# Moving the head sums of the RWKV bonus behind the prep, with the products parked in DRAM

## The chip, the core and the metric

The kernel runs on one core of a Trainium2 chip. TensorE (PE) multiplies, VectorE (DVE) and ScalarE (ACT) do elementwise work and evict the accumulators, GpSimd (POOL) and SyncE (SP) here mostly start DMAs; ACT starts DMAs as well, from the same queue that holds its compute instructions. Each engine takes its instructions strictly in the order in which they were laid down, so an instruction that waits holds up everything behind it on that engine. The metric is device microseconds of one execution; lower is better.

## The reference, cut to what matters

The block has an RWKV-7 time mixing branch, a gated recurrent branch, cross-attention and a gated convolutional FFN, for 512 positions of width 1024. The change touches one line of the time mixing, the `bonus`:

```python
p = p + (token_shift(p) - p) * mu
r, k, v = p[..., :c0], p[..., c0:c1], p[..., c1:c2]
...
k = k * (1.0 + (a - 1.0) * k_a)
...
y = rwkv7_recurrence(r, decay, k, v, -kk, kk * a)
mean = jnp.mean(y, axis=-1, keepdims=True)
var = jnp.mean(jnp.square(y - mean), axis=-1, keepdims=True)
y = ((y - mean) * lax.rsqrt(var + LNX_EPS)).reshape(bsz, s, A_WIDTH) * lnx_g + lnx_b
bonus = jnp.sum(r * k * r_k, axis=-1, keepdims=True) * v
return (y + bonus.reshape(bsz, s, A_WIDTH)) * g
```

Per head of 64 channels and per position, the products r\*k\*r_k are added up to one number, which scales v. Eight heads lie in four pairs, each pair being a tile of 128 channels (partitions) by 512 positions.

## The kernel before

Activations lie with channels on partitions and positions along the free axis. Every dense product is done in three matmuls of a split in high and low parts (L160, L161, L162), so a block of 128 output columns with 1024 inputs is 24 matmuls 128x512, written to an accumulator `in_ps`. There are 38 such blocks in the input projection: the first 14 make r, k, v and the low-rank inputs of the time mixing, then come 16 gate blocks (`in_ps22` on, evicted by ACT into `gs`, stored to `dG`), then 8 blocks of the other branch. Their weights stream from DRAM on SP's queue (`win_r`), and ACT (`win_h`, L114) and DVE (`win_l`, L115) split them; three split blocks are held at a time, so `win_h` of a block waits until PE is done with the block three earlier. Three `in_ps` accumulators are held at a time.

Between these blocks the scheduler, which lays each engine's order down when the program is built, sets the time mixing's own work:

- **Prep**, for each of the four head pairs j: `prep` (two small products psw and psa, then sigmoid, a scan `L`, exponentials), `prep2` (norm of k through a head sum `ss`, then the decayed rows `AK` and `KBt`), `scores` (32 matmuls 64x128, L605, in four accumulators, evicted by eight DVE operations L609 and L610 into `BZ` and `AK`, and half of it stored to `dM` by SP), and `bonus`. psw, psa, ss, the four `sc` and `bo` take turns in four accumulator slots (`prw`).
- `bonus(j)` before the change, L585 to L591: DVE multiplies r, r_k and k in place in `pr`; `sum_exact` (L154 to L157) splits the product on ACT (`bo_h`) and DVE (`bo_l`) and adds over each head with two matmuls against a block matrix of ones into `bo`; DVE multiplies by v; ACT adds `lnx_b`; a DMA from ACT's queue stores the tile in `dBo`, where the group norm reads it much later (L821).
- **The block inverse**: two DMAs bring the diagonal blocks of all heads from `dM` back as `Nm` (L654), and 31 steps of two DVE operations each (L660, L661) invert them in `Zt`; the result goes through DRAM (`dZt`, `dZ`) into `ZA` and `BZ`; then come small matmuls `zh` and `zo`, and the scan over eight chunks. PE goes through gate blocks meanwhile. The tiles of the inverse lie in the memory that the prep's pool `pp` has just given back.

A third stream rides along: POOL starts 512 KB accumulating DMAs `dS` in DRAM for the later FFN (L425), each released by a given matmul of a given block (`sum_behind`): one each behind the first products of blocks `in_ps27`, `in_ps28` and `in_ps29`, none in `in_ps30` to `in_ps37`.

Of the kernel before, what the change touches and what calls it, by code (L numbers as in the profile page):

```python
# [9 lines left out]
F32 = mybir.dt.float32  # L10
F32R = mybir.dt.float32r
AF = mybir.ActivationFunctionType
ALU = mybir.AluOpType
# [4 lines left out]
P = 128  # L18
T = 512
# [6 lines left out]
NPAIR = NH // 2  # L26
# [27 lines left out]
def hybrid_block_kernel(ctx: ExitStack, tc: tile.TileContext, xT_d, mT_d, pv_d, cst_d, win_d, wk_d, wv_d,  # L54
                        lup_d, gup_d, rga_d, rgx_d, wba_d, wbb_d, wmix_d, wq_d, wo_d, wfi_d, wfo_d, out_d):
    nc = tc.nc
    V, S, PE = nc.vector, nc.scalar, nc.tensor
# [12 lines left out]
    def mm_ps(name):  # L70
        return pmm.tile([P, T], F32, tag="mm", name=name)

    def rw_ps(name, pool=None, tag="rw", **kw):
        return (pool or prw).tile([P, T], F32, tag=tag, name=name, **kw)
# [9 lines left out]
    def par(name, i, n=1):  # L84
        o = PV[name][0]
        return pv[:, o + i:o + i + n]
# [63 lines left out]
    def sum_exact(ps, blocks, src, pool, tag, name):  # L150

        hi = pool.tile(list(src.shape), F32R, tag=tag, name=f"{name}_h", bufs=2)
        lo = pool.tile(list(src.shape), F32R, tag=tag, name=f"{name}_l", bufs=2)
        S.copy(hi, src)  # L154
        V.tensor_tensor(lo, src, hi.bitcast(F32), ALU.subtract)
        PE.matmul(ps, blocks, hi, start=True, stop=False)
        PE.matmul(ps, blocks, lo, start=False, stop=True)  # L157
# [36 lines left out]
    bonesr = cp.tile([P, P], F32R, name="bonesr")  # L194
# [72 lines left out]
    with tc.tile_pool(name="p0", bufs=1, reuse_waits="tile") as p0:  # L267
# [36 lines left out]
        for m in range(KB):  # L304
            ps = rw_ps(f"k_ps{m}") if 3 <= m < 6 else mm_ps(f"k_ps{m}")
# [93 lines left out]
    dBo = dr.tile([4, P, T], F32, name="dBo")  # L399
# [82 lines left out]
    vT = pa.tile([P, NPAIR, T], F32, name="vT")  # L482
# [4 lines left out]
    tp = tp_ctx.enter_context(tc.tile_pool(name="tp", bufs=1, reuse_waits="tile"))  # L487
# [28 lines left out]
    def inproj(i):  # L516
        ps = mm_ps(f"in_ps{i}")
        dense(ps, uin, lambda kb: (h2[:, 0, kb, :], h2[:, 1, kb, :]), KB, NSUM.get(i, 0))
        return ps

    def evac_shift(ps, blk, out):
        q = pp.tile([P, T], F32, tag="q", name=f"q{blk}", bufs=2)
        V.tensor_copy(q[:, 0:1], qb[:, blk:blk + 1])
        S.activation(q[:, 1:T], ps[:, 0:T - 1], AF.Identity, scale=par("mu", blk), bias=par("b_in", blk))
        V.scalar_tensor_tensor(out, ps, omu[:, blk:blk + 1], q, ALU.mult, ALU.add)  # L525
# [17 lines left out]
    def prep(j):  # L543
        sl = slice(j * P, (j + 1) * P)
        psw, psa = rw_ps(f"psw{j}"), rw_ps(f"psa{j}")
        for i, ps in enumerate((psw, psa)):
            PE.matmul(ps, lhi[:, i, sl], pwa[i], start=True, stop=False)
            PE.matmul(ps, llo[i][:, sl], pwa[i], start=False, stop=True)
        L = pp.tile([P, T], F32, tag="L", name=f"L{j}")
        tab(L, psw, AF.Sigmoid, bias=par("w0", j))  # L550
        at = pp.tile([P, T], F32, tag="at", name=f"at{j}")
        tab(at, psa, AF.Sigmoid, bias=par("a0", j))
        V.tensor_tensor_scan(L, smask, L, 0.0, ALU.mult, ALU.add)
        Pp = pp.tile([P, NC, HD + 1], F32, tag="Pp", name=f"Pp{j}")
        V.memset(Pp[:, :, 0:1], 1.0)
        tab(Pp[:, :, 1:], L.rearrange("p (c t) -> p c t", t=HD), AF.Exp, scale=-C0)
        tab(L, L, AF.Exp, scale=C0)
        V.tensor_copy(PC[:, j, :], Pp[:, :, HD])
        return at, L, Pp

    def prep2(j, pk, pr, at, Pi, Pp):
        c3 = lambda a: a.rearrange("p (c t) -> p c t", t=HD)
        kk = pp.tile([P, T], F32, tag="kk", name=f"kk{j}")
        S.activation(kk, pk, AF.Copy, scale=par("k_k", j))
        sq = pp.tile([P, T], F32, tag="q", name=f"sq{j}", bufs=2)
        S.activation(sq, kk, AF.Square)
        ps = rw_ps(f"ss{j}")
        sum_exact(ps, bonesr, sq, tp, "xb", f"ss{j}")
        tab.rsqrt(sq, ps, 1.0, eps[:, 2:3])
        V.scalar_tensor_tensor(kk, sq, 1e12, kk, ALU.min, ALU.mult)  # L570
        jc = slice(j * NC, (j + 1) * NC)
        for e in range(2):
            hs = half[e]
            V.scalar_tensor_tensor(AK[hs, e, jc, 0:HD], c3(kk)[hs], -1.0, Pp[hs, :, 0:HD], ALU.mult, ALU.mult)
        V.tensor_tensor(kk, kk, at, ALU.mult)
        V.tensor_tensor(KBt[:, j, 1::2, :], c3(kk), c3(Pi), ALU.mult)
        S.activation(at, at, AF.Identity, scale=par("k_a", j), bias=oka[:, j:j + 1])
        V.tensor_tensor(pk, pk, at, ALU.mult)
        V.tensor_tensor(KBt[0:HD, j, 2::2, :], c3(pk)[0:HD], c3(Pi)[0:HD], ALU.mult)
        V.tensor_tensor(KBt[HD:P, j, 0:2 * NC:2, :], c3(pk)[HD:P], c3(Pi)[HD:P], ALU.mult)  # L580
        for e in range(2):
            hs = half[e]
            V.tensor_tensor(AK[hs, e, jc, HD:P], c3(pr)[hs], Pp[hs, :, 1:], ALU.mult)

    def bonus(j, pk, pr):  # L585
        V.scalar_tensor_tensor(pr, pr, par("r_k", j), pk, ALU.mult, ALU.mult)
        ps = rw_ps(f"bo{j}")
        sum_exact(ps, bonesr, pr, tp, "xb", f"bo{j}")
        V.tensor_tensor(pr, ps, vT[:, j, :], ALU.mult)
        S.activation(pr, pr, AF.Identity, bias=par("lnx_b", j))  # L590
        nc.scalar.dma_start(dBo[j], pr)  # L591

# [3 lines left out]
    def scores(j):  # L598
        for e in range(2):
            hs, oh = half[e], half[1 - e]  # L600
            for cg in range(2):
                ps = rw_ps(f"sc{j}_{e}_{cg}")
                i0 = j * NC + cg * 4
                for i in range(4):
                    PE.matmul(ps[:, i * P:(i + 1) * P], kb_cols(j, e, cg * 4 + i), AK[hs, e, i0 + i, :],  # L605
                              start=True, stop=True)
                p3 = ps.rearrange("p (c t) -> p c t", t=P)
                m3 = scmask.unsqueeze(1).to_broadcast([P, 4, P])
                V.tensor_tensor(BZ[hs, i0:i0 + 4, :], p3[hs], m3[hs], ALU.mult)  # L609
                V.tensor_tensor(AK[oh, e, i0:i0 + 4, :], p3[oh], m3[oh], ALU.mult)  # L610
            with tc.high_priority(offset=1000000):
                nc.sync.dma_start(dM[e * 32 + j * NC:e * 32 + (j + 1) * NC].rearrange("i s t -> s i t"),
                                  BZ[hs, j * NC:(j + 1) * NC, 0:HD])

    def gate_block(b):
        ps = inproj(22 + b)
        sg = tp.tile([P, T], F32, tag="st", name=f"gs{b}", bufs=2)
        tab(sg, ps, AF.Sigmoid, bias=par("b_in", 22 + b))
        nc.scalar.dma_start(dG[b], sg)

    for jp in range(2):
        js = (2 * jp, 2 * jp + 1)
        pks, prs = {}, {}
        for j in js:
            pks[j] = pp.tile([P, T], F32, tag="pk", name=f"pk{j}", bufs=2)
            evac_shift(inproj(4 + j), 4 + j, pks[j])
        for j in js:
            prs[j] = pp.tile([P, T], F32, tag="pr", name=f"pr{j}", bufs=3)
            evac_shift(inproj(j), j, prs[j])
        for j in js:  # L630
            evac_shift(inproj(8 + j), 8 + j, vT[:, j, :])
        for j in js:
            if j == 3:
                for i in IN_REST[:NEARLY]:
                    gate_block(i - 22)
            at, L, Pp = prep(j)
            prep2(j, pks[j], prs[j], at, L, Pp)
            scores(j)
            bonus(j, pks[j], prs[j])

    pp_ctx.close()
    pq_ctx = ExitStack()
    pq = pq_ctx.enter_context(tc.tile_pool(name="pq", bufs=1, reuse_waits="tile"))
    YB = pq.tile([P, 4, T], F32, name="YB")


    with tc.tile_pool(name="pz", bufs=1, reuse_waits="tile") as pz:
# [216 lines left out]
    def px_scan(b, xb, ga, gx):  # L864
# [5 lines left out]
        V.tensor_tensor(xb, xb, gx, ALU.mult)  # L870
        V.tensor_tensor_scan(YB[:, b, :], ga, xb, 0.0, ALU.mult, ALU.add)

    def py_block(b):
        ps = inproj(18 + b)
        ge = tp.tile([P, T], F32, tag="st", name=f"ge{b}", bufs=2)
        with tc.high_priority():
            tab(ge, ps, AF.Gelu_apprx_tanh, bias=par("b_in", 18 + b))
            V.tensor_tensor(YB[:, b, :], YB[:, b, :], ge, ALU.mult)

# [26 lines left out]
    for b in range(4):  # L906
        yb = YB[:, b, :]
        with tc.high_priority():
# [17 lines left out]
    for m in range(KB):  # L926
        ga = pm.tile([P, T], F32, tag="ga", name=f"gta{m}")
# [26 lines left out]
    for m in range(KB):  # L954
        xin = pm.tile([P, T], F32, tag="xin", name=f"xin{m}")
        nc.scalar.dma_start(xin, xT_d[:, m, :])
        ps = mm_ps(f"mix_ps{m}")
# [23 lines left out]
    pk = pk_ctx.enter_context(tc.tile_pool(name="pk", bufs=1, reuse_waits="tile"))  # L981
# [73 lines left out]
    pr = ctx.enter_context(tc.tile_pool(name="pr", bufs=1, side="right", reuse_waits="tile"))  # L1055
# [17 lines left out]
    for m in order:  # L1073
        ps = mm_ps(f"co_ps{m}")
# [343 lines left out]
```

## Time and profile before

| | |
|---|---|
| median of 3 runs | 911.82 us (911.26 to 913.13) |
| the profiled execution: its own time | 909.73 us |
| its span, first to last instruction | 908.0 us |
| PE busy | 890.5 us, 98% |
| DVE busy | 687.4 us, 76% |
| ACT busy | 510.4 us, 56% |
| granted TensorE clock, mean | 0.998 |

The median is 2.09 us above the profiled execution's own time, and that is 1.73 us above its span. A row of the timeline gives start, duration, engine, line, operation, output<-inputs, and in brackets idle time of the engine before it with what ended it. A matmul's shown duration overlaps the next one's, so the distance between two starts says more than the duration.

### The profile page before, as it was taken

How to read it: one execution, taken by the hardware profiler on the slowest of the kernel's cores; microseconds unless marked ns; L12 is line 12 of the kernel's file. 1: busy time of each engine (PE TensorE's matmuls, PEld its weight loads, DVE VectorE, ACT ScalarE, POOL GpSimd, SP SyncE). 2: the span in 40 equal slices, each digit the busy share in tenths (PEclk: the TensorE clock that was granted, in tenths of full speed). 3: DMA queues.
4: the chain of work that ended last, by engine and by line, in shares of the span. 5: the costliest groups of instructions: out<-in, count | busy, mean ns of one | idle time of the engine just before them, and what ended most of it. 6: DMA issues, size and time to landing. Idle time of an engine off the chain costs nothing. (4 is left out here: it accounts for less than half of the span.)

```text
span 908.0 us, 15914 instructions
## 1 busy us (share of the span) xinstructions
PE 890.5 (98%) x6218; PEld 776.1 (85%) x6218; DVE 687.4 (76%) x1096; ACT 510.4 (56%) x779; POOL 129.3 (14%) x159
## 2 busy tenths in 40 slices
PE   7999999999999999999999999999999999999996
PEld 6988877788877777887887778999999999999996
DVE  7884598776957585776565568788998888999674
ACT  6674675542236675234454446765665556767663
POOL 0102222010011212001112211111111111201100
PEclk9999999999999999999999999999999999999999
DMA  8878899667499749858788868898989998998963
GB/s 276 277 263 230 186 237 208 179 165 206 139 205 246 167 106 194 258 180 223 210 243 190 177 152 185 240 273 247 280 249 290 258 316 251 248 277 222 269 197 93
DMA packets 102411, 200.07 MB, mean 220 GB/s; under 512 B 25344, under 2 KB 36736, under 8 KB 102272
## 3 DMA queue, kind: packets, MB, share of 16 engines
q1 hardware_dynamic: 69504, 119.75, 41.0%
q0 software_dynamic: 25504, 67.38, 36.8%
q10 hardware_dynamic: 7328, 11.92, 3.9%
q8 instruction: 49, 0.80, 0.3%
q14 instruction: 26, 0.21, 0.1%
HBM read 187.75 MB, written 77.59 MB: 292 GB/s over the span
## 5 line engine op out<-in xcount | busy, mean ns | idle before, releaser
L126 ACT CAST wfi_h<-wfi_r 128x1024 fp32r<-128x1024 f32 x77 | 81.0, 1052 | 76.8 <-PE fx_ps L161 21.1
L160 PE MATMUL in_ps<-hT,win_h 128*128 128x512 f32 x304 | 121.9, 402 | 0.8 <-DVE pr L525 0.7
L162 PE MATMUL in_ps<-hT,win_l 128*128 128x512 f32 x304 | 120.8, 398 | 0.0
L161 PE MATMUL in_ps<-hT,win_h 128*128 128x512 f32 x304 | 120.6, 398 | 0.0
L127 DVE TENSOR_TENSOR wfi_l<-wfi_r,wfi_h 128x1024 fp32r<-128x1024 f32 x77 | 94.0, 1221 | 23.5 <-ACT wfi_h L126 23.3
L425 POOL DMA_DIRECT2D dS<-in_wfi x66 | 66.5, 1044 | 267.0 <-PE in_ps L160 132.4
L114 ACT CAST win_h<-win_r 128x1024 fp32r<-128x1024 f32 x38 | 39.8, 1048 | 71.9 <-PE in_ps L161 70.9
L115 DVE TENSOR_TENSOR win_l<-win_r,win_h 128x1024 fp32r<-128x1024 f32 x38 | 46.4, 1221 | 32.6 <-ACT win_h L114 32.5
L160 PEld LDWEIGHTS in_ps<-hT,win_h 128*128 128x128 f32 x304 | 57.0, 187 | 15.6 <-DVE pr L525 1.1
L161 PEld LDWEIGHTS in_ps<-hT,win_h 128*128 128x128 f32 x304 | 57.0, 188 | 14.0 <-issue 0.7
L162 PEld LDWEIGHTS in_ps<-hT,win_l 128*128 128x128 f32 x304 | 57.0, 187 | 13.9 <-issue 0.2
L461 POOL DMA_DIRECT2D dOs<-in_wfo x54 | 39.9, 804 | 186.0 <-PE fx_ps L160 50.9
L1245 DVE TENSOR_TENSOR wfo_l<-wfo_r,wfo_h 128x1024 fp32r<-128x1024 f32 (+1 forms) x39 | 47.2, 1210 | 13.6 <-ACT wfo_h L1244 13.5
L1244 ACT CAST wfo_h<-wfo_r 128x1024 fp32r<-128x1024 f32 (+1 forms) x39 | 40.4, 1038 | 28.2 <-PE oyz_ps L161 9.8
L161 PE MATMUL fx_ps<-hr,wfi_h 128*128 128x256 f32 x176 | 49.7, 282 | 0.0
L162 PE MATMUL fx_ps<-hr,wfi_l 128*128 128x256 f32 x176 | 49.7, 282 | 0.0
L160 PE MATMUL ox_ps<-go,wfo_h 128*128 128x256 f32 x176 | 49.6, 282 | 0.1
L160 PE MATMUL fyz_ps<-hq,wfi_h 128*128 128x256 f32 x176 | 49.3, 280 | 0.4 <-ACT p L1173 0.4
L160 PE MATMUL fx_ps<-hq,wfi_h 128*128 128x256 f32 x176 | 49.5, 281 | 0.0
L160 PE MATMUL fx_ps<-hr,wfi_h 128*128 128x256 f32 x176 | 49.4, 281 | 0.0
L162 PE MATMUL ox_ps<-go,wfo_l 128*128 128x256 f32 x176 | 49.3, 280 | 0.0
L161 PE MATMUL ox_ps<-go,wfo_h 128*128 128x256 f32 x176 | 49.3, 280 | 0.0
(418 smaller groups left out, 2727.8 us busy)
## 6 DMA issues: line engine op xcount, KB each, us to landing
dS<-in_wfi POOLq DMA_DIRECT2D x66, 512.0 KB, 8.4
wfi_r<-dS SPq DMA_DIRECT2D x44, 512.0 KB, 6.9
win_r<-in_win SPq DMA_DIRECT2D x38, 512.0 KB, 5.0
wfi_r<-in_wfi SPq DMA_DIRECT2D x33, 512.0 KB, 5.6
dS<-dS POOLq DMA_DIRECT2D x22, 512.0 KB, 5.7
dOs<-in_wfo POOLq DMA_DIRECT2D x12, 512.0 KB, 7.8
wv_r<-in_wv SPq DMA_DIRECT2D x8, 512.0 KB, 4.9
dG<-gs ACTq DMA_DIRECT2D x16, 256.0 KB, 2.6
```

The lines of the kernel that those rows point to most:

```text
L114: S.copy(hi[:, o:o + n], raw[:, o:o + n])
L115: V.tensor_tensor(lo[:, o:o + n], raw[:, o:o + n], hi[:, o:o + n].bitcast(F32), ALU.subtract)
L126: S.copy(hi, raw)
L127: V.tensor_tensor(lo, raw, hi.bitcast(F32), ALU.subtract)
L160: first = PE.matmul(ps, lh, rh, start=start, stop=False, **kw)
L161: PE.matmul(ps, lh, rl, start=False, stop=False, **kw)
L162: PE.matmul(ps, ll, rh, start=False, stop=stop, **kw)
L425: return lambda: nc.gpsimd.dma_start(s(out), src, **kw)
L461: yield lambda k=k, w=w, src=src: nc.gpsimd.dma_start(dO[n, m][:, k * P:(k + w) * P], src, **kw)
L1244: S.copy(hi[:, :n], raw[:, :n])
L1245: V.tensor_tensor(lo[:, :n], raw[:, :n], hi[:, :n].bitcast(F32), ALU.subtract)
```

## The change

`bonus` is cut in two. `bonus_terms(j)` stays in the prep: DVE's product, and then a DMA from ACT's queue that stores the bare product in `dBo[j]`. The new `bonus(j)` is called for all four pairs after the prep's pool is closed and ahead of the inverse: a DMA from ACT's queue brings the product back into a new tile `bt` (two buffers, tag "ga", which the prep's low-rank weights `llo` hold until the last psw and psa), and then the same sum, product with v, bias and store as before follow. So four stores and four loads of 256 KB are added; the number of matmuls and of DVE and ACT computations stays the same. As `bt` has two buffers, the load of `bt2` waits until the final store from `bt0` has landed, and `bt3` until that from `bt1` has.

```diff
-    def bonus(j, pk, pr):
+    def bonus_terms(j, pk, pr):
+
         V.scalar_tensor_tensor(pr, pr, par("r_k", j), pk, ALU.mult, ALU.mult)
+        nc.scalar.dma_start(dBo[j], pr)
+
+    def bonus(j):
+        bt = tp.tile([P, T], F32, tag="ga", name=f"bt{j}", bufs=2)
+        nc.scalar.dma_start(bt, dBo[j])
         ps = rw_ps(f"bo{j}")
-        sum_exact(ps, bonesr, pr, tp, "xb", f"bo{j}")
-        V.tensor_tensor(pr, ps, vT[:, j, :], ALU.mult)
-        S.activation(pr, pr, AF.Identity, bias=par("lnx_b", j))
-        nc.scalar.dma_start(dBo[j], pr)
+        sum_exact(ps, bonesr, bt, tp, "xb", f"bo{j}")
+        V.tensor_tensor(bt, ps, vT[:, j, :], ALU.mult)
+        S.activation(bt, bt, AF.Identity, bias=par("lnx_b", j))
+        nc.scalar.dma_start(dBo[j], bt)
...
             scores(j)
-            bonus(j, pks[j], prs[j])
+            bonus_terms(j, pks[j], prs[j])
 
     pp_ctx.close()
     pq_ctx = ExitStack()
     pq = pq_ctx.enter_context(tc.tile_pool(name="pq", bufs=1, reuse_waits="tile"))
     YB = pq.tile([P, 4, T], F32, name="YB")
+    for j in range(NPAIR):
+        bonus(j)
```

The diff moves instructions all through the prep, since the scheduler lays the order anew. Three places matter. The first is PE at the end of block `in_ps29`, after the last pair's scores (`sc3`). Before, the last bonus sum (`bo3`) was over long ahead of this place:

```order
L160 MATMUL in_ps28_2735<-hT2_0_89,win_h20_2738 128x512
L156 MATMUL bo3_1727<-bo3_h_1728,bonesr_80 128x512
L161 MATMUL in_ps28_2735<-hT2_1_90,win_h20_2738 128x512
L162 MATMUL in_ps28_2735<-hT2_0_89,win_l20_2739 128x512
L160 MATMUL in_ps28_2735<-hT2_0_89,win_h20_2738 128x512
L161 MATMUL in_ps28_2735<-hT2_1_90,win_h20_2738 128x512
L162 MATMUL in_ps28_2735<-hT2_0_89,win_l20_2739 128x512
L157 MATMUL bo3_1727<-bo3_l_1729,bonesr_80 128x512
```

Now the sum of pair 2 begins right at the end of `in_ps29`, and that of pair 3 nine matmuls later:

```order
L162 MATMUL in_ps29_2782<-hT2_0_89,win_l21_2786 128x512
L156 MATMUL bo2_1732<-bo2_h_1733,bonesr_80 128x512
L160 MATMUL in_ps30_2817<-hT2_0_89,win_h22_2820 128x512
L161 MATMUL in_ps30_2817<-hT2_1_90,win_h22_2820 128x512
L157 MATMUL bo2_1732<-bo2_l_1734,bonesr_80 128x512
L162 MATMUL in_ps30_2817<-hT2_0_89,win_l22_2821 128x512
L160 MATMUL in_ps30_2817<-hT2_0_89,win_h22_2820 128x512
L161 MATMUL in_ps30_2817<-hT2_1_90,win_h22_2820 128x512
L162 MATMUL in_ps30_2817<-hT2_0_89,win_l22_2821 128x512
L160 MATMUL in_ps30_2817<-hT2_0_89,win_h22_2820 128x512
L156 MATMUL bo3_1744<-bo3_h_1745,bonesr_80 128x512
```

Pairs 0 and 1 have moved from the prep to just behind `sc3` (bo0 at once, the second matmul of bo1 in `in_ps28`), so six of the eight bonus matmuls that stood ahead of `sc3` are now behind it.

The second place is ACT from the split of `win_h22` on, in the changed kernel (`gs5`, `gs6`, `gs7` are the evictions of blocks `in_ps27`, `in_ps28`, `in_ps29`; "DMA" rows are DMAs that ACT issues):

```order
L237 ACTIVATE gs5_2744<-in_ps27_2712,pv_75 128x512
L596 ACTIVATE bt0_1706<-bt0_1706,pv_75 128x512
L625 DMA dG_712<-gs5_2744 128x512
L597 DMA dBo_713<-bt0_1706 128x512
L596 ACTIVATE bt1_1718<-bt1_1718,pv_75 128x512
L114 CAST win_h23_2854<-win_r23_2852 128x1024
L597 DMA dBo_713<-bt1_1718 128x512
L592 DMA bt2_1730<-dBo_713 128x512
L237 ACTIVATE gs6_2779<-in_ps28_2747,pv_75 128x512
L625 DMA dG_712<-gs6_2779 128x512
L592 DMA bt3_1742<-dBo_713 128x512
L154 CAST bo2_h_1733<-bt2_1730 128x512
```

What moved: two stores and two loads now stand in ACT's order ahead of the split `bo2_h`, which PE needs; before, one store stood in this stretch.

The third is DVE where the inverse begins. Before, its steps followed one another from the first; now the product of pair 3's sum with v stands behind the second step:

```order
L595 TENSOR_TENSOR bt2_1730<-bo2_1732,vT_745 128x512
L155 TENSOR_TENSOR bo3_l_1746<-bt3_1742,bo3_h_1745 128x512
L668 TENSOR_TENSOR zz_1760<-Zt_1758,Nm_1757 128x1
L669 TENSOR_REDUCE Zt_1758<-zz_1760 128x1
L668 TENSOR_TENSOR zz_1760<-Zt_1758,Nm_1757 128x4
L669 TENSOR_REDUCE Zt_1758<-zz_1760 128x2
L595 TENSOR_TENSOR bt3_1742<-bo3_1744,vT_745 128x512
L668 TENSOR_TENSOR zz_1760<-Zt_1758,Nm_1757 128x9
```

So the third and all later steps of the inverse stand behind the bonus of pair 3.

## Prediction

> **What bounds the kernel now.** I read the page first, then the stretches of the time mixing, then who waits for whom on PE.
>
> ```profile
> span 908.0 us, 15914 instructions
> PE 890.5 (98%) x6218; PEld 776.1 (85%) x6218; DVE 687.4 (76%) x1096; ACT 510.4 (56%) x779; POOL 129.3 (14%) x159
> ```
>
> In the windows the columns are length, then busy time (and count) of PE, PEld, DVE, ACT, POOL, then granted clock, DMA share and GB/s.
>
> ```profile
> 100.00:120.00 20.00, 19.45 (x101) 15.95 (x100) 15.71 (x23) 14.45 (x19) 3.75 (x4) 1.00 0.87 210
> 120.00:140.00 20.00, 19.24 (x96) 14.88 (x95) 18.96 (x33) 13.50 (x18) 6.04 (x6) 1.00 0.97 219
> 140.00:160.00 20.00, 19.48 (x85) 15.10 (x84) 16.69 (x26) 13.55 (x18) 4.45 (x5) 1.00 0.92 205
> 160.00:180.00 20.00, 19.77 (x102) 15.93 (x101) 16.30 (x24) 10.73 (x16) 0.00 (x0) 1.00 0.66 193
> 180.00:200.00 20.00, 20.00 (x103) 16.29 (x102) 16.68 (x23) 9.40 (x12) 1.87 (x2) 1.00 0.54 130
> 200.00:220.00 20.00, 20.00 (x88) 16.05 (x87) 10.10 (x31) 6.55 (x8) 1.14 (x1) 1.00 0.92 238
> ```
>
> PE is the bound from end to end. In these windows it idles only in the prep, 2.06 us from 100 to 180, and from 180 to 220, where the bonus now goes, not at all, while DVE and ACT have room there (10.10 and 6.55 of 20). The number of matmuls doesn't change, so the time changes only by what PE waits less or more. The same matmul cadence holds throughout:
>
> ```profile
> 187.21 0.39 PE L161 MATMUL in_ps<-hT,win_h 128*128 128x512 f32 x1
> 187.44 0.39 PE L162 MATMUL in_ps<-hT,win_l 128*128 128x512 f32 x1
> 187.75 3.68 PE L605 MATMUL sc<-AK,KBt 64*128 64x128 f32 x32
> 191.36 0.50 PE L160 MATMUL in_ps<-hT,win_h 128*128 128x512 f32 x1
> ```
>
> One 128x512 matmul starts 0.233 us after another, a block of 24 takes 5.6 us, and the last pair's scores (sc3) start at 187.75 and hold PE 3.6.
>
> **The waits in the prep that can go.**
>
> ```profile
> 119.30 0.47 PE L156 MATMUL bo<-bo_h,bonesr 128*128 128x512 f32 x1 [0.55 <-DVE AK L610]
> 133.74 0.50 PE L160 MATMUL in_ps<-hT,win_h 128*128 128x512 f32 x1 [0.67 <-DVE pr L525]
> 144.75 0.49 PE L157 MATMUL bo<-bo_l,bonesr 128*128 128x512 f32 x1 [0.35 <-DVE bo_l L155]
> 145.41 0.50 PE L160 MATMUL in_ps<-hT,win_h 128*128 128x512 f32 x1 [0.17 <-DVE pk L525]
> 171.49 0.50 PE L157 MATMUL bo<-bo_l,bonesr 128*128 128x512 f32 x1 [0.23 <-DVE bo_l L155]
> ```
>
> The brackets add up to 1.97; since a shown duration of 0.4 overlaps the next start by 0.16, each hides up to 0.16 more, so about 2.7 in all. The first is a wait for an accumulator slot that a score eviction gives back: in the new order psw of pair 1 stands at that spot and waits for the same slot, so it stays (0.65), and ss of pair 1 comes right behind psa and waits for the third slot, about 0.7 by the spacing of two evictions (0.7 each). The waits at 133.74 and 145.41 are for accumulators that DVE, nearly full there (18.96 of 20), evicts late; without two bo_l and two products with v (about 0.65 each) DVE comes earlier, and I leave 0.3 of those 1.1. The two on bo_l go. So 2.7 plus some 0.7 of smaller slips becomes 0.65 + 0.7 + 0.3, rounded: **-2.1 us** (bounds -0.8, if the slots only pass the waits on, and -3.4, if all goes).
>
> By this PE is at sc3 at 187.75 - 2.1 + 0.7 = 186.4: six bonus matmuls fewer stand ahead of it and nine of in_ps27 more, three matmuls of 0.233. Is DVE there in time? Its chain for pair 3 starts with psw, now about 3.5 earlier (2.1, and six matmuls fewer ahead of it), takes bo0_l in between (0.65), and at3 has slipped behind win_h21 on ACT, which waits for PE; I get KBt at 185.8, 0.6 ahead. A miss would cost up to 1; I take 0.
>
> **The bonus beside the inverse.** Behind sc3 the rows that price it are these, of DVE and ACT:
>
> ```profile
> 189.30 0.68 DVE L609 TENSOR_TENSOR BZ<-sc,cst 64x512 f32<-64x512 f32 x1
> 194.19 0.68 DVE L610 TENSOR_TENSOR AK<-sc,cst 64x512 f32<-64x512 f32 x1
> 196.01 1.23 DVE L115 TENSOR_TENSOR win_l<-win_r,win_h 128x1024 fp32r<-128x1024 f32 x1 [0.28 <-ACT win_h L114]
> 198.49 0.69 DVE L589 TENSOR_TENSOR pr<-bo,vT 128x512 f32<-128x512 f32 x1 [0.64 <-PE bo L157]
> 194.93 1.05 ACT L114 CAST win_h<-win_r 128x1024 fp32r<-128x1024 f32 x1 [7.44 <-PE in_ps L161]
> 195.89 0.61 ACT L154 CAST bo_h<-pr 128x512 fp32r<-128x512 f32 x1
> 199.21 0.73 ACT L590 ACTIVATE pr<-pr,pv 128x512 f32<-128x512 f32 x1 [2.13 <-DVE pr L589]
> ```
>
> The eight evictions (189.30 to 194.87) start 1.4 earlier less pr3's product that now stands ahead of them: they end at 193.0. DVE then does bt0's product (to 193.7), win_l22 (1.23, to 194.9) and bo1_l (to 195.6). PE, after sc3 at 190.0, two bo0, three in_ps, bo1_h and 18 in_ps, is at bo1's second matmul at 195.4: **+0.4** with the hand-over (0 to 1.0). It then has 9 + 24 matmuls and reaches bo2's first at 203.7.
>
> bo2_h on ACT needs the load of bt2, and that waits for bt0's store to land. bt0's product done at 193.7, bias on ACT to 194.4, store issued at about 195.2; bt1's store behind win_h23, which waits for PE to end in_ps28 (197.9), at about 199.0. How long do 256 KB on ACT's queue take here? These are issues of the windows 196:198, 199:201 and 202:206 (kind, queue, count, KB, us to landing), the two POOL rows that start dS, and the queues' shares in 198:202 and 202:206:
>
> ```profile
> dG<-gs ACTq DMA_DIRECT2D x1, 256.0 KB, 7.5
> dBo<-pr ACTq DMA_DIRECT2D x1, 256.0 KB, 6.7
> dG<-gs ACTq DMA_DIRECT2D x1, 256.0 KB, 7.0
> Nm<-dM SPq DMA_DIRECT2D x1, 256.0 KB, 13.9
> ...
> 195.66 1.16 POOL L425 DMA_DIRECT2D dS<-in_wfi  x1 [8.68 <-PE in_ps L160]
> 201.78 1.14 POOL L425 DMA_DIRECT2D dS<-in_wfi  x1 [4.96 <-PE in_ps L160]
> ...
> q0 software_dynamic: 230, 0.46, 98.5%
> q10 hardware_dynamic: 8, 0.02, 1.2%
> ...
> q1 hardware_dynamic: 1828, 0.74, 66.3%
> q10 hardware_dynamic: 278, 0.51, 33.7%
> ```
>
> A dS (q0) holds nearly all of the engines for some 4 us; ACT's queue (q10) stands still and then shares with Nm. The dS are tied to PE (first matmul of in_ps28 and in_ps29), so they come 3 earlier in the new kernel, at 192.5 and 198.6, and so does Nm, at 195.6. The new stores and loads fall into the same crowd as the three rows above. With about 7 each, bt0's store lands at 202 to 203 and bt2's load at about 208.6; bo2_h takes 0.61, and PE goes on at 209.3 instead of 203.7: **+5.4**. Bounds: 0, with transfers as short as this row, from 170:180, where no dS runs,
>
> ```profile
> dBo<-pr ACTq DMA_DIRECT2D x1, 256.0 KB, 2.0
> ```
>
> and +9.5, with 9 each as the longest dS of this stretch (9.2 in its issue row). I take 5.4 since the new transfers lie in the crowd, not beside it. A page of the Trainium skill, "DMA: Bandwidth & Descriptors", section "Queues, rings and completion order", says that each engine goes round-robin between the queues that have work, packet by packet. The trace doesn't agree for 198 to 202, where dG and dBo were queued and q10 got 1.2%. By that rule both transfers would be much shorter than 7 and most of the +5.4 would go; the sum goes by the rows.
>
> bt3's load goes out when bt1's store has landed (205 to 206) and lands at 210 to 211; ACT does bo2_h, win_h24, gs7 first and has bo3_h at about 211.9, PE comes to it at 211.4: **+0.5** (0 to 3). Waiting behind bt2 and bt3 on ACT are gs6 and gs7 (accumulators for in_ps31 and later) and win_h24 (needed for in_ps32): PE, itself standing, needs them more than 8 us later, so 0.
>
> **The inverse.** The first step ran at 212.45 once Nm had landed; PE's first zh, which needs ZA from it, is this row:
>
> ```profile
> 212.45 0.16 DVE L660 TENSOR_TENSOR zz<-Zt,Nm 128x1 f32<-128x1 f32 x1 [3.22 <-DMA Nm<-dM]
> 266.45 1.19 PE L687 MATMUL zh<-ZA,BZ 32*32 32x32 f32 x32
> ```
>
> Zh had no idle ahead of it, so the slack was 0 or more. The third step (zz of 9) began 0.8 after the first, at 213.2. Now it waits for bt3's product: PE's last bo3 at 214.2, plus 0.5 and 0.69, 215.5, or 2.3 later. PE itself is 4.2 later and meets zh three matmuls (0.7) earlier in its order, so the inverse gains 1.2 of slack: **0** (0 to 2, if Nm with 1 MB more beside it lands 3 later than I think). What follows is the same work on a saturated PE.
>
> **Sum:** -2.1 + 0.4 + 5.4 + 0.5 = +4.2. The profiled execution's 909.73 (span 908.0 + 1.73 around it) becomes 913.9; the three runs' median lies 2.09 above that execution, so I forecast 911.82 + 4.2 = **916.0 us**.
>
> **Rivals.** (1) *The transfers are short.* Stores and loads of 2.0: bt0's store lands at 197.2, bt2 is issued at 199.1, lands at 201.1, bo2_h is done at 201.8, ahead of PE's 203.7; bt3 likewise. Then only -2.1 + 0.4 is left: 910.1, not slower. For it: the 2.0 row, and that DMAs of ACT go out a little earlier against the dS; against it: three rows of 6.7 to 7.5 at this spot. It decides from the point where store and load together take under 8 us. (2) *The crowd is worse,* 9 each with 1 MB added beside Nm: +9.5 in place of 5.4 and +1 more on bo3: +9.3, 921.1. (3) *The prep gains nothing,* the slots and DVE's order passing each wait on to the next instruction, or KBt late for sc3 (at3 behind win_h21): +6.3, 918.1. (4) *The inverse is late:* Nm lands past 216 and zh waits 2: 918.
>
> **Chances.** Forecast (a wait of 3 to 8 at bo2 and bo3) 0.60, own range 913 to 918.5; rival 1 0.20; rivals 2, 3 and 4 together 0.20. A measurement here tells some 0.2% (1.8 us) from no change. Faster by more: half of rival 1 and a little of better prep, 0.13. Within: the other half and the forecast's low end, 0.22. Slower: 0.65. Range 910.0 to 920.0, from rival 1 to the edge of rival 2.
>
> **What would show it.** PE idle in 100 to 180 down from 2.06 to about 1, no row of bo there. On PE one wait of 3 to 8 us ahead of a bo row L156 released by ACT's bo_h, near 209, with ACT's own idle ahead of bo_h released by a DMA bt<-dBo. bt loads and stores in 195 to 212 with 6 us or more to landing. The inverse's third step 2 to 3 us later and no idle ahead of zh. I am wrong if PE has no idle over 1 us in 195 to 215, if the loads land in under 4, or if the time moves at zh or later.

## The result: slower by 0.8%, and the profile after

| | before | after |
|---|---|---|
| median | 912.15 us (909.87 to 913.13, 6 runs) | 919.04 us (918.17 to 920.48, 6 runs) |
| after / before, 95% interval | | 1.008 (1.0066 to 1.0094) |
| profiled execution: its own time, span | 909.73, 908.0 us | 918.73, 917.0 us |

The change costs 6.9 us of the median; the prediction had +4.2. A second series of runs of the same kernel, e8 below, gave 921.94 (918.11 to 924.04, 4 runs) against 910.06, a ratio of 1.0125 (1.0104 to 1.0145). One run of e4 below took 1083.63 us at a granted clock of 0.755, a slow state of the chip, and counts in no ratio. From the page of the changed kernel, total work first:

```profile
span 917.0 us, 15941 instructions
PE 889.7 (97%) x6218; PEld 775.7 (85%) x6218; DVE 687.2 (75%) x1096; ACT 510.0 (56%) x779; POOL 129.3 (14%) x159
```

PE does the same 6218 matmuls in the same 890 us; the 9.0 us that the span is longer are idle time and slower matmuls. The windows of the prep and of the place where the sums now stand (columns as in the prediction; the granted clock is the third from the right):

```profile
100.00:120.00 20.00, 19.46 (x101) 15.78 (x100) 16.94 (x25) 14.05 (x18) 4.48 (x5) 1.00 0.85 212
120.00:140.00 20.00, 19.43 (x100) 15.35 (x99) 19.56 (x33) 11.16 (x14) 5.13 (x6) 1.00 0.93 194
140.00:160.00 20.00, 19.86 (x88) 15.73 (x87) 15.86 (x25) 15.28 (x21) 4.63 (x6) 1.00 0.98 228
160.00:180.00 20.00, 20.00 (x103) 16.56 (x103) 14.95 (x21) 11.63 (x16) 0.00 (x0) 1.00 0.64 201
180.00:200.00 20.00, 20.00 (x103) 16.16 (x102) 16.49 (x24) 7.10 (x9) 3.01 (x3) 1.00 0.73 189
200.00:220.00 20.00, 13.52 (x52) 10.54 (x51) 8.09 (x24) 6.43 (x9) 0.00 (x0) 0.83 0.80 214
```

In the prep PE now idles 1.25 us instead of 2.06. From 200 to 220, where it had no idle at all, it stands still for 6.48 us, and the granted clock there is 0.83. PE's timeline shows both losses, the standstill ahead of `bo2` and what the matmuls behind it take:

```profile
202.58 0.40 PE L162 MATMUL in_ps<-hT,win_l 128*128 128x512 f32 x1
209.46 0.79 PE L156 MATMUL bo<-bo_h,bonesr 128*128 128x512 f32 x1 [6.48 <-ACT bo_h L154]
210.05 0.63 PE L160 MATMUL in_ps<-hT,win_h 128*128 128x512 f32 x1
210.48 0.63 PE L161 MATMUL in_ps<-hT,win_h 128*128 128x512 f32 x1
...
212.61 0.44 PE L162 MATMUL in_ps<-hT,win_l 128*128 128x512 f32 x1
212.89 0.39 PE L160 MATMUL in_ps<-hT,win_h 128*128 128x512 f32 x1
213.12 0.39 PE L156 MATMUL bo<-bo_h,bonesr 128*128 128x512 f32 x1
```

Seven starts from 210.05 to 212.61 lie 0.43 apart instead of 0.233. From 209.46 to 212.89 PE does eight matmuls where it would have done 14.7: (3.43 - 8 x 0.233) = 1.6 us lost to the clock. The wait at `bo2` is the one the prediction named, and ACT's timeline has its cause:

```profile
193.78 0.33 ACTq L597 DMA_DIRECT2D dBo<-bt  x1
197.24 0.33 ACTq L597 DMA_DIRECT2D dBo<-bt  x1
201.95 0.33 ACTq L592 DMA_DIRECT2D bt<-dBo  x1
202.32 0.69 ACT L237 ACTIVATE gs<-in_ps,pv 128x512 f32<-128x512 f32 x1 [4.09 <-DMA dBo<-bt]
208.79 0.62 ACT L154 CAST bo_h<-bt 128x512 fp32r<-128x512 f32 x1 [5.78 <-DMA dG<-gs]
```

The store of `bt0` goes out at 193.78, and the load of `bt2`, which needs its buffer, can go out only at 201.95, 8.2 later; ACT stands behind it for 4.09. The load lands 6.8 later, and only then can ACT make `bo2_h`. (The bracket of the last row names `dG<-gs`; what the cast reads is `bt2`.) Behind it `bo3` doesn't wait any more, and the inverse is held for the product of `bt3`, as foreseen, without harm to `zh` on PE:

```profile
215.17 0.69 DVE L595 TENSOR_TENSOR bt<-bo,vT 128x512 f32<-128x512 f32 x1 [1.66 <-PE bo L157]
215.78 0.16 DVE L668 TENSOR_TENSOR zz<-Zt,Nm 128x9 f32<-128x9 f32 x1
...
271.03 0.66 PE L695 MATMUL zh<-ZA,BZ 32*32 32x32 f32 x15
```

To see where the rest of the 9.0 is, I cut each profiled execution at the first start of PE's groups: first and last `sc` (the prep from the first scores on), first `yb_ps` (the inverse and the chunk scan are over), first `q_ps` and first `co_ps` (the attention between them). Times in us; the experiments' rows are used further down.

| kernel | to first sc | sc | last sc to yb | yb to q | q to co | co to end | span |
|---|---|---|---|---|---|---|---|
| before | 115.3 | 75.9 | 167.3 | 91.1 | 67.6 | 390.8 | 908.0 |
| **after** | 114.0 | 74.8 | 174.8 | 91.1 | 70.2 | 392.1 | 917.0 |
| after again (e8) | 115.4 | 74.8 | 176.2 | 92.7 | 69.7 | 390.5 | 919.3 |
| e1 four buffers | 115.5 | 74.9 | 175.0 | 91.7 | 67.7 | 392.2 | 917.0 |
| e2 no DRAM | 115.6 | 72.8 | 173.9 | 100.0 | 69.3 | 390.8 | 922.4 |
| e3 traffic only | 115.0 | 78.1 | 164.8 | 92.6 | 67.6 | 390.7 | 908.8 |
| e4 sums later | 113.4 | 74.8 | 169.2 | 91.1 | 70.4 | 391.5 | 910.4 |
| e5 order held | 115.4 | 74.8 | 170.6 | 91.8 | 72.5 | 390.8 | 915.9 |
| e6 before, sums later | 116.7 | 75.9 | 167.4 | 91.2 | 67.6 | 391.2 | 910.0 |
| e7 held, sums later | 115.8 | 74.8 | 166.8 | 91.6 | 69.5 | 391.8 | 910.3 |
| e9 own order, sums later | 115.3 | 74.8 | 167.7 | 91.3 | 68.0 | 390.7 | 907.8 |
| e10 held, both later | 114.6 | 74.8 | 166.8 | 91.9 | 68.3 | 392.7 | 909.1 |
| e11 attention sum later | 115.3 | 74.8 | 175.2 | 91.1 | 68.6 | 391.5 | 916.5 |

The prep gives back 1.1, the stage of the inverse takes 7.5 more, and 2.6 more go in the attention, 260 us behind the change, where nothing in the diff differs. One and the same kernel (after and e8) differs by 1.4 to 1.6 us between its two rows in the start, in "yb to q" and in the last stage, so differences of that size there say nothing; "sc" repeats within 0.1 in before and e6, which have the same order on PE, and in after, e4, e5, e7, e8, e10 and e11, which share another.

### The profile page after: what moved, and what is told of

The parts are those of the page before. It is cut to its first block, busy times and chain, and to the rows that moved or that the text cites. A ratio compares the mean times of both kernels' runs of the same rounds, so it can differ in the third digit from the quotient of the medians.

```text
span 917.0 us, 15941 instructions
## 1 busy us (share of the span) xinstructions
PE 889.7 (97%) x6218; PEld 775.7 (85%) x6218; DVE 687.2 (75%) x1096; ACT 510.0 (56%) x779; POOL 129.3 (14%) x159
## 5 line engine op out<-in xcount | busy, mean ns | idle before, releaser
L160 PE MATMUL fx_ps<-hq,wfi_h 128*128 128x256 f32 x176 | 49.9, 284 | 0.0
L160 PE MATMUL ox_ps<-go,wfo_h 128*128 128x256 f32 x176 | 49.8, 283 | 0.0
L161 PE MATMUL fx_ps<-hq,wfi_h 128*128 128x256 f32 x176 | 49.4, 280 | 0.0
```

Of the source, the lines that this page charges most:

```text
L160: first = PE.matmul(ps, lh, rh, start=start, stop=False, **kw)
L161: PE.matmul(ps, lh, rl, start=False, stop=False, **kw)
```

## The experiments

Three theories at the outset. A: the loss is the round trip of `bt0` and `bt1` through DRAM that `bt2` and `bt3` wait for. B: it is the traffic of the added stores and loads. C: it is the place, the sums beside the inverse in an order laid anew, whatever the way of the products. e1 to e4 ran beside one series of the kernel before (910.22), e5 to e8 beside a second (910.06), e9 to e11 beside a third (910.18).

**e1, four buffers.** No load waits for a store any more.

```diff
-        bt = tp.tile([P, T], F32, tag="ga", name=f"bt{j}", bufs=2)
+        bt = tp.tile([P, T], F32, tag=("ga", "gx")[j // 2], name=f"bt{j}", bufs=2)
```

> The changed kernel, but bt2 and bt3 take two other buffers (tag gx) that are free here, so that no load of a product waits for a store of a sum; the four stores and four loads stay. Theory A (PE waits at bo2 because bt2's load stands behind bt0's store, both in a crowded stretch, 6.5 us, and then runs at half clock for 1.5): no PE wait over 1.5 us at a bo row, no half clock near 210, and 910 to 912 us. Theory B (the 2 MB more of DMA traffic slow the weights or Nm): still 917 to 920. Theory C (sums beside the inverse cost by their place on PE and DVE, whatever they read from): still 916 or more.

919.46 us, ratio 1.0097 (1.0071 to 1.0122). The wait at `bo2` is gone and nothing is won: the scheduler, which now thinks `bt2` and `bt3` early, lays the order anew (six matmuls fewer ahead of `zh` than in after), and PE's timeline shows the loss at `zh`:

```profile
267.43 1.91 PE L695 MATMUL zh<-ZA,BZ 32*32 32x32 f32 x32 [3.93 <-DMA ZA<-dZt]
```

The window around it, with the clock at 0.83:

```profile
260.00:280.00 20.00, 15.75 (x130) 10.77 (x130) 6.05 (x10) 5.49 (x8) 4.89 (x5) 0.83 1.04 239
```

**e2, no DRAM.** The products stay on the chip in four tiles, without the added stores and loads; the sums stand beside the inverse.

```diff
+    bts = {}
...
-        V.scalar_tensor_tensor(pr, pr, par("r_k", j), pk, ALU.mult, ALU.mult)
-        nc.scalar.dma_start(dBo[j], pr)
+        bts[j] = tp.tile([P, T], F32, tag=("gx", "ga")[j // 2], name=f"bt{j}", bufs=2)
+        V.scalar_tensor_tensor(bts[j], pr, par("r_k", j), pk, ALU.mult, ALU.mult)
...
-        bt = tp.tile([P, T], F32, tag="ga", name=f"bt{j}", bufs=2)
-        nc.scalar.dma_start(bt, dBo[j])
+        bt = bts[j]
```

> The sums stand beside the inverse as in the changed kernel, but the products stay in on-chip buffers (tags gx and ga): no store and load of products. A: no wait at bo2, 909.5 to 911.5 us, the gain of 1.8 in the prep alone. B: the same, about 910. C: 916 or more.

923.5 us, ratio 1.0137 (1.0115 to 1.016), the slowest of all. Neither `bo` nor `zh` waits; PE stands at `zo`, `yb_ps`, `ya_ps` and `mix_ps` instead (2.6, 2.0, 1.7 and 1.3 us), in an order laid anew once more. Its largest loss, 8.9 us, lies between the first `yb_ps` and the first `q_ps`, which every other kernel passes in 91 to 93; it was not followed further. Theory A in its simple form, that the time comes back with the round trip, falls with e1 and e2.

**e3, the traffic alone.** The bonus stays in the prep as before; the products are also stored to a second buffer and loaded back into `bt` tiles that nothing reads.

```diff
+    dBx = dr.tile([4, P, T], F32, name="dBx")
...
         V.scalar_tensor_tensor(pr, pr, par("r_k", j), pk, ALU.mult, ALU.mult)
+        nc.scalar.dma_start(dBx[j], pr)
...
+        bt = tp.tile([P, T], F32, tag=("ga", "gx")[j // 2], name=f"bt{j}", bufs=2)
+        nc.scalar.dma_start(bt, dBx[j])
```

> The kernel before with the same added traffic and nothing moved: each product is also stored to DRAM in the prep, and four loads of 256 KB bring them back after the prep, read by nobody. A: within 1.5 us of the kernel before (911 to 913.5). B: 915 or more. C: as before.

910.49 us, ratio 1.0007 (0.9991 to 1.0022): four stores and four loads of 256 KB cost nothing as long as nobody waits for them. Theory B falls, with a reservation: the scheduler laid the order anew here too (the last scores stand ten matmuls later than before), and the four loads land by 197, ahead of most of the crowd. So e3 acquits the amount of the traffic, not its place. e10 below, which has the same added traffic in the order of after and takes as long as before, agrees.

**e4, the sums of the FFN later.** The changed kernel, with the three `dS` transfers of blocks 27 to 29 moved to 32 to 34; the order on all five engines stays that of after.

```diff
-            22: 2, 23: 1, 27: 1, 28: 1, 29: 1, 15: 4, 16: 4, 17: 4, 18: 4, 19: 4, 20: 3, 21: 2}
+            22: 2, 23: 1, 32: 1, 33: 1, 34: 1, 15: 4, 16: 4, 17: 4, 18: 4, 19: 4, 20: 3, 21: 2}
```

> The changed kernel, but the three accumulating DMAs dS that go with in_ps27 to in_ps29 go with in_ps32 to in_ps34 instead; PE's order there is the same, bo2 still behind in_ps29. A with the dS as the cause of the long transfers: bt0's store and bt2's load take 2 to 4 us each, the wait at bo2 falls to 0 to 3 us, 910.5 to 915 us. If Nm's many small packets hold ACT's queue just as well: the wait stays at 5 or more, 916 to 919. B and C: 917 or more.

914.93 us, ratio 1.0045 (1.0022 to 1.0068); the profiled execution, 912.28, lies 2.65 under the median. The queues in 194:202 (share of 16 engines last) and the issues of `bt0`'s store, `bt1`'s store and `bt2`'s load (count, KB, us to landing), of after and then of e4:

```profile
q0 software_dynamic: 266, 0.51, 53.0%
q10 hardware_dynamic: 430, 0.78, 27.2%
...
dBo<-bt ACTq DMA_DIRECT2D x1, 256.0 KB, 8.1
dBo<-bt ACTq DMA_DIRECT2D x1, 256.0 KB, 5.3
bt<-dBo ACTq DMA_DIRECT2D x1, 256.0 KB, 6.8
```

```profile
q1 hardware_dynamic: 4275, 1.06, 65.8%
q10 hardware_dynamic: 542, 0.99, 45.4%
...
dBo<-bt ACTq DMA_DIRECT2D x1, 256.0 KB, 2.2
dBo<-bt ACTq DMA_DIRECT2D x1, 256.0 KB, 3.2
bt<-dBo ACTq DMA_DIRECT2D x1, 256.0 KB, 4.9
```

Without the `dS` (q0) the two stores take 2.2 and 3.2 instead of 8.1 and 5.3 and the load 4.9 instead of 6.8, `Nm` lands 5.2 to 7.6 after its issue instead of 13.2 to 16.1, and the waits at `bo` in 195:290 shrink to these, with the clock at 1.00 throughout (total, times, longest, in us):

```profile
PE bo L156 <- ACT bo_h L154: 2.1, 2, 1.8
```

So the crowd at this place sets the length of the wait, as the prediction had it, and the crowd is the `dS`. The stage of the inverse takes 5.6 less than in after; the attention still takes 70.4.

**e5, four buffers in the order of after.** To part the wait from the laying of the order, every engine's order in the stretch that e1 had changed is held as in after by edges between neighbours; only the loads of `bt2` and `bt3` go out early.

```diff
-        bt = tp.tile([P, T], F32, tag="ga", name=f"bt{j}", bufs=2)
+        bt = tp.tile([P, T], F32, tag=("ga", "gx")[j // 2], name=f"bt{j}", bufs=2)
...
+        for row in HELD.values():
+            names = [f"I-{n}" for n in row.split()]
+            for one, two in zip(names, names[1:]):
+                tc.add_manual_dep(made[two], one, mybir.DependencyInfo(
+                    mybir.DependencyClass.NoSync, mybir.DependencyReason.DATA), reason="order held")
```

> Four buffers as in e1, but the order of after is held on all five engines; only the loads of bt2 and bt3 go out early, so nothing waits for a round trip. Theory W (what the changed kernel loses is the wait at bo2 and the slow clock behind it, 6.5 + 1.5 us, and e1 was slow only because the order was laid anew): no bo row waits over 1 us, the clock in 200 to 220 stays at 1.00, the inverse starts with Nm at 212 to 213 as before, zh waits under 1, and the time is 919.0 - 8.0 = 911 (910 to 912), the same as before within 0.2%. Rival R (the inverse has too little slack for a PE that comes early, whatever the order): the wait moves to zh with 2 to 4 us and a low clock behind it, 914 or more.

916.92 us, ratio 1.0076 (1.006 to 1.0092): rival R, the loss moves to `zh`. No `bo` waits over 0.6, but `zh` does, although the inverse begins even earlier than before (211.96 against 212.45); these rows of the timeline are the inverse's first step on DVE and PE's `zh`:

```profile
211.96 0.16 DVE L743 TENSOR_TENSOR zz<-Zt,Nm 128x1 f32<-128x1 f32 x1 [3.59 <-DMA Nm<-dM]
...
266.03 1.19 PE L770 MATMUL zh<-ZA,BZ 32*32 32x32 f32 x32 [0.90 <-DMA ZA<-dZt]
```

And the windows around it:

```profile
264.00:268.00 4.00, 3.10 (x39) 2.36 (x38) 3.96 (x6) 1.95 (x4) 2.98 (x3) 0.92 1.01 151
268.00:272.00 4.00, 4.00 (x14) 2.88 (x13) 0.01 (x1) 0.59 (x1) 0.00 (x0) 0.66 1.14 179
272.00:276.00 4.00, 4.00 (x40) 2.35 (x40) 0.68 (x1) 0.69 (x1) 0.49 (x1) 1.00 1.18 270
```

PE now comes to `zh` at 265.13, 1.3 earlier than before (266.45), and the inverse's result isn't there: a wait of 0.9 and a clock of 0.66 in the next 4 us. So the way from `Nm` over 31 steps and two DRAM trips to `ZA` was nearly a second limit in the kernel before: `ZA` comes at 266.03 here and PE stood at `zh` at 266.45 there, so the slack was about 0.4 us by these two executions. (In before's own trace the first part of `ZA`, issued at 258.5, took 7.0 to land: 0.9 before PE came.) The stage takes 170.6: of the 8.0 that after spends above the 166.8 of e7 below, 4.2 are back and 3.8 are lost at `zh`. The attention, 72.5 here, loses again as in after, by a longer wait (us in total, times, longest) and with a low clock behind it:

```profile
PE sc_ps L1099 <- ACT ex L1106: 2.9, 1, 2.9
...
480.00:484.00 4.00, 4.00 (x19) 3.54 (x18) 1.57 (x7) 1.21 (x4) 0.22 (x1) 0.70 0.48 169
```

**e6, before with the sums later.** The kernel before with e4's edit, its order unchanged.

```diff
-            22: 2, 23: 1, 27: 1, 28: 1, 29: 1, 15: 4, 16: 4, 17: 4, 18: 4, 19: 4, 20: 3, 21: 2}
+            22: 2, 23: 1, 32: 1, 33: 1, 34: 1, 15: 4, 16: 4, 17: 4, 18: 4, 19: 4, 20: 3, 21: 2}
```

> The kernel before, with the same move of three dS sums as in e4 (from in_ps27 to 29 to in_ps32 to 34); the bonus is computed in the prep as before. Theory W: before has no wait between 180 and 220 that the sums could cause, so the time stays within 1.5 us of before's median in this call, though Nm lands 5 or more us sooner. Rival S (the sums cost time there in any kernel, and e4 gained by that and not by the shorter wait at bo2): 3 to 4 us faster than before, as e4 is faster than after.

911.04 us, ratio 1.0009 (1.0 to 1.0018). The sums cost the kernel before nothing where they are; e4's gain is the shorter wait and the clock that stays at 1.00 behind it.

**e7, e5 and e4 together.** Diff: both of theirs.

> e5 and e4 together: no round trip ahead of bo2, the order of after held, the three sums later, so Nm lands near 207 and the inverse has 5 us more. Theory W: no wait at bo and none at zh, the same as e5 within 1 us, 910 to 911.5. Rival R: e7 faster than e5 by 2 us or more, since only here the inverse is early enough for a PE that comes early. If the 2.6 us that the attention stage took longer in after and e4 belong to the later bonus itself, e7 shows them too and comes to 913.

911.51 us, ratio 1.0021 (1.0011 to 1.0032). Neither `bo` nor `zh` waits; the inverse's first step and PE's `zh`:

```profile
207.97 0.15 DVE L743 TENSOR_TENSOR zz<-Zt,Nm 128x1 f32<-128x1 f32 x1
...
264.76 1.19 PE L770 MATMUL zh<-ZA,BZ 32*32 32x32 f32 x32
```

5.4 us faster than e5 with only the sums moved. The profiles show 3.8 of that in the stage of the inverse, so e5's loss there was the late inverse; another 3.0 lie in the attention (69.5 against 72.5). The stage of the inverse takes 166.8, 0.5 less than before, and with the prep's 1.1 the change is worth 1.6 us up to there. The attention takes 1.9 more and eats it.

**e8, the changed kernel again.** No edit.

> The changed kernel once more, beside the others on the same chip, for a second profile. The wait at bo2 is there again with 5 to 8 us and a clock of 0.5 to 0.8 for 3 us behind it; median 919.0 (918 to 920). Open is the stage of the attention, from the first q to the first co matmul, 67.6 us in before and 70.2 in the first profile of after: if the later bonus causes it, 70 again; if it was an accident of that execution, 68.

921.94 us, above the 918 to 920 expected. The wait at `bo2` is 6.8, and the clock is at 0.50 until 216 at least:

```profile
206.00:208.00 2.00, 0.00 (x0) 0.00 (x0) 0.00 (x0) 0.00 (x0) 0.00 (x0) 0.64 1.25 235
...
211.21 0.79 PE L156 MATMUL bo<-bo_h,bonesr 128*128 128x512 f32 x1 [6.84 <-ACT bo_h L154]
...
214.00:216.00 2.00, 2.00 (x6) 1.59 (x5) 1.16 (x6) 0.72 (x1) 0.00 (x0) 0.50 0.77 229
```

Its stage is 9.4 longer than e7's (6.8 and 2.6), against 8.0 in the first profile (6.5 and 1.5). The attention takes 69.7: not an accident of one execution.

**e9, e1 with the sums later.** Diff: e1's and e4's.

> e1 (four buffers, the order laid anew, where zh waited 3.9 us) with the three dS sums later as in e4. Theory R' (the wait at bo2 and the wait at zh are two limits that follow one another, both set by the crowd of dS): Nm lands near 204 and not at 213, the inverse ends 5 or more us earlier, zh waits under 0.5, the clock stays at 1.00, and the attention stage takes 67.7 as in e1, so the time is before's median less 1.6, 908 to 910. Rival C (the newly laid order itself costs time): 913 or more, with the loss at other places than zh.

The profile agrees with theory R': no wait at `bo` or `zh`, the inverse starts at 203.95, the stage takes 167.7 (e1: 175.0), and that run took 909.64. PE has the order of e1, so the 7.3 us that e1's stage is longer are the wait at `zh` (3.9) and the slow clock behind it, not the new order. The median doesn't agree: 913.08, the time that rival C had named, ratio 1.0024 (1.0005 to 1.0043), the runs spread from 909.2 to 919.5. What the slower ones lose isn't seen in the one profile, of a run of 909.64, and stays open.

**e10 and e11, the sum in the attention later.** e10 is e7, e11 the changed kernel, each with this edit: two `dS` behind the second head's first q block go two weight steps later.

```diff
-            if kb * nsum % nkb < nsum:
+            if (kb - skip) * nsum % nkb < nsum:
...
-            dense(ps, uq, lambda kb: (hx[:, 0, kb, :], hx[:, 1, kb, :]), KB, nsum + i * (nsum > 0))
+            dense(ps, uq, lambda kb: (hx[:, 0, kb, :], hx[:, 1, kb, :]), KB, nsum + i * (nsum > 0),
+                  2 if (hd, i) == (1, 0) else 0)
```

> e7 with two more dS sums moved, those behind the first 24 matmuls of the second head's first q block: each two weight steps (1.4 us) later. In all five profiles of kernels with the order of after the second load of K goes out 0.4 to 0.6 us ahead of the first of these and takes 6 to 8 us, in the profiles of before, e3, e6 and e1 about 1 us ahead and takes 4.3 to 4.9. Theory K (the attention stage loses its 2 to 5 us there because this sum overtakes the load): q to co takes 67.6 instead of 69.5, the wait of sc_ps for ex goes, and the time is 1.5 to 2 us under e7, at or a little under before: 908.5 to 910. Rival: the load of K is late for another reason, the stage takes 69 to 70 again and the time is e7's.

> The changed kernel with only that second move: the two sums in the attention stage two weight steps later, all else as in after, the wait at bo2 included. Theory K: the stage from q to co takes 67.6 instead of 69.7 to 70.2, and the time is 2 to 2.6 us under after's 919 to 922: 916.5 to 919.5, ratio to before 1.007 to 1.010; the wait at bo2 stays at 6 to 7 us. Rival: 70 again, 919 to 922.

e10: 910.75, ratio 0.9997 (0.9988 to 1.0007), the same as before and a little over the 908.5 to 910 expected. Theory C falls with it, since the sums stand beside the inverse here too. The 1.6 gained up to the chunk scan is gone again in the three stages behind it (0.8, 0.7 and 1.9 more than before); the first is of the size by which after and e8 differ, the last little more, so whether a gain is left is not shown. e11: 918.77, ratio 1.0079 (1.0056 to 1.0103), beside the 1.008 and 1.0125 of after: its median shows no clear gain, only the stage does. The place is this wait of after, on PE's timeline:

```profile
479.07 0.39 PE L1024 MATMUL sc_ps<-K,q 128*128 128x256 f32 x1 [1.81 <-ACT ex L1031]
```

`ex` is late because K is. The view of the tile `kvK` gives its two loads, in before:

```profile
DMA to landing us min/median/max: 4.3/4.7/5.2
```

In after:

```profile
DMA to landing us min/median/max: 5.7/6.3/6.8
```

And in e11:

```profile
DMA to landing us min/median/max: 4.7/5.3/6.0
```

The second load is short again with the `dS` out of its way, `sc_ps` no longer waits for `ex` in either kernel, and the stage takes 68.3 instead of 69.5 and 68.6 instead of 69.7 to 70.2. Theory K, that a `dS` overtakes the second load, holds for 1.1 to 1.6 us; 0.7 to 1.0 over the 67.6 of before, which was forecast, remain. In after the first load is the 5.7, in before the 5.2, issued at the same distance from the first q; it is 5.6 or more in every profile with the order of after, and 5.3 or less in before, e1, e3, e6 and e9. Why is not settled. The half microsecond is enough to push the second load into the `dS`, which is tied to PE; these are the two issues in after, 0.5 apart (in before 0.8):

```profile
467.65 0.38 ACTq L998 DMA_DIRECT2D kvK<-dK  x1
...
468.17 0.71 POOL L425 DMA_DIRECT2D dS<-dS  x1 [17.65 <-PE q_ps L160]
```

## Why the prediction was right, and where its sum was not

The direction, the mechanism and the place were right, and 919.0 lies in the range of 910 to 920, half a microsecond beyond the likeliest case's own range of 913 to 918.5. That the time fell into the range is in part luck: two losses were left out of the sum, the range reached to 920 for another reason (a worse crowd), and the second series, 921.9, lies outside it. By its steps:

- **"The waits in the prep that can go", -2.1, and "+0.4" at bo1.** Together -1.7. The first sum is off: 2.7 and 0.7 become 0.65 + 0.7 + 0.3, which is a gain of 1.75 and not 2.1, and with it -1.35 together. Measured -1.6, in e7, where nothing hides it (74.8 + 166.8 against 75.9 + 167.3). bo1 didn't wait at all, and idle fell to 1.25, about the 1 named as a sign.
- **The wait at `bo2`, "+5.4".** 6.48, 6.8 and 6.2 in the three profiles that have it. PE went on at 209.46; the prediction said 209.3, but its own two times, 203.7 and 209.3, are 5.6 apart and not 5.4, and PE came at 203.0. The two transfers took 8.2 and 6.8 instead of 7 each. That the `dS` make them long was shown by e4.
- **`bo3`, "+0.5".** No wait: PE came to it late and slowly.
- **"The inverse: 0".** In after `zh` doesn't wait, and the third step began at 215.78 (said: 215.5). But the reason given, 1.2 us of slack gained, was the wait's own doing: take the wait away and the inverse is the limit (e5).
- **Rival 1's price, 910.1, was wrong.** It took the wait away and left the rest alone. e5 is the nearest case, and it took 916.9. The limit behind the limit was not priced.
- **The step that failed is the sum itself,** which counted a standstill as its own length and ended with "the same work on a saturated PE". Two terms are missing. One is the clock behind the standstill: 1.5 to 2.6 us. The other is the attention, +2.1 to 2.6, through the load of K.

With the measured terms the profiled pair adds up, the 1.5 being what e7's stage leaves over beside the wait (the count of matmuls above gave 1.6): -1.6 + 6.5 + 1.5 + 2.6 = 9.0 (a start 1.3 earlier and 1.3 lost behind the attention cancel). The median's +6.9 in one series and +11.9 in the other lie on both sides of it; the three times that the slow clock behind `bo2` was profiled it cost 1.5, 2.6 and 2.2 (e11: 175.2 - 166.8 - 6.2), so it alone can spread the runs by a microsecond.

The first missing term is seen in these windows of after, which have the clock in the third column from the right:

```profile
205.00:210.00 5.00, 0.54 (x1) 0.50 (x2) 0.56 (x1) 1.21 (x2) 0.00 (x0) 0.59 1.15 291
210.00:212.00 2.00, 2.00 (x6) 1.56 (x5) 1.74 (x3) 1.45 (x3) 0.00 (x0) 0.50 0.33 117
212.00:214.00 2.00, 2.00 (x8) 1.59 (x8) 1.41 (x6) 0.72 (x1) 0.00 (x0) 0.82 0.81 258
214.00:216.00 2.00, 2.00 (x10) 1.60 (x10) 0.79 (x3) 0.10 (x1) 0.00 (x0) 1.00 0.59 234
```

It sinks while PE stands, is at half when PE goes on, and back at full from 214. The Trainium skill, "TensorE: Matmul & The Clock Gate", section "Part 1: The HAM clock gate", says that an idle window of about 3.4 us halves the array's clock, that about 3.4 us of work restore it, and that the window runs freely. After agrees (6.48 us idle, then 0.43 between starts for some 3.4 us), and so do the differing losses of e8 and e11. But the clock doesn't wait for 3.4 us of idle: in e8 PE stood from 204.4, and 0.64 in 206:208 puts the fall at about 206.6, 2.2 later. e5 agrees still less: there 0.9 us of idle, followed by a `zh` block of 32x32 matmuls, was enough for a clock of 0.66 in 268:272, while waits of 1.8 in e4 between full matmuls left it at 1.00. That the small matmuls count as little activity would fit; it wasn't tried.

## What to carry to other kernels

A wait is worth its length only if nothing stands close behind it: before moving work for the sake of 2 us, look at the slack of every chain that ends on the same engine, here `Nm` to `ZA`, since an engine that comes earlier runs into the next one. Reusing a buffer through a store and a load adds both transfers to the critical path, at the crowd's length (8.2 + 6.8 us) and not at that of a quiet stretch (a store of 2.0, a load of 2.6 in after); the same amount of traffic with nobody waiting for it cost nothing (e3). Price a standstill of PE of several microseconds with the half clock behind it, and hold the order when one edit is to be judged alone: where the scheduler laid it anew, the effect of the edit and that of the new order could not be told apart, in e1 not before e9, in e2 not at all.

## What the runs showed of the hardware that I had not expected

- A standstill of 6.2 to 6.8 us is followed by matmuls at 0.43 us instead of 0.233 for 3 us or more; 0.9 us ahead of a block of 32x32 matmuls did the same (e5), 1.8 us between full ones did not (e4).
- 512 KB accumulating transfers from DRAM to DRAM stretch the transfers beside them: `Nm` (256 KB in small pieces) lands after 13.2 to 16.1 us with them in after and after 5.2 to 7.6 without in e4, two 256 KB stores after 8.1 and 5.3 with them and after 2.2 and 3.2 without.
- A load that lands 0.5 us later, in a stage that the change doesn't touch, let such a transfer overtake the next load: PE waited 1.8 us there (after) and 2.9 (e5), and moving that transfer away gave 1.1 to 1.6 back.
